# Layer 2's forget queries and keys by column blocks, with two smaller moves to ScalarE

## The chip, the cores and the metric

One core of a Trainium2 chip runs the whole program. The metric is the device time of one execution in microseconds (us). Engine names are those of the profile: PE multiplies matrices, PEld loads its stationary operand, DVE is the vector engine, ACT the scalar engine, POOL the general-purpose one, SP the queue from which transfers are issued.

## The reference, cut to what matters

Two layers on 256 tokens of 1024 features, in single precision. Each layer has a mixer with two groups of eight heads (sparse attention with grouped keys, and forgetting attention), then a squared-ReLU MLP; each is wrapped in norms.

```python
h = _rms_norm(x, g_pre_mix[l])
parts = jnp.split(h @ w_in[l], split_at, axis=-1)
nq, kc, vc, ksel, vsel, kwin, vwin, gates, fq, fk, fv, ff = parts
o_nsa = _nsa_mixer(...)                       # compressed, selected and window branches, gated
o_fox = _fox_mixer(heads(fq, 8), heads(fk, 8), heads(fv, 8), ff, b_forget[l])
mix = jnp.concatenate([o_nsa, o_fox], axis=-1) @ w_out[l]
x = x + _rms_norm(mix, g_post_mix[l])
h = _rms_norm(x, g_pre_mlp[l])
y = jnp.square(jax.nn.relu(h @ w_up[l])) @ w_down[l]
x = x + _rms_norm(y, g_post_mlp[l])
```

In the forgetting group, a head's logits are `q . k / 8 + cum[q] - cum[k]` under a causal mask, where `cum` is the running sum of log-sigmoids of `ff`; softmax of them multiplies `fv`. `fq` and `fk`, 512 columns each of `w_in`, are what the change is mostly about.

## The kernel before, in words

**Products in three parts.** Every large product of `h` and a weight is made of three matmuls. `Weights.get` brings a weight unit of 128 x 1024 numbers (tile `wraw`), and splits it into a rounded high part `whi` (a copy by ACT) and a low part `wlo` (a subtraction by DVE). The activations lie turned (features on partitions) as `xT`, also a high and a low part, side by side in one tile: `xT[0]` high, `xT[1]` low, `xT[2]` both, 2 x 256 columns for each of the eight feature groups k. A product is high x high + high x low + low x high (`mm3`).

**The input projection** goes chunk by chunk through `w_in` (`CHUNKS`): 0 to 2 and 5 are made with tokens on partitions (`in_chunk`), chunk 3 (`fq`) and chunk 4 (`fk`) turned, features on partitions, by `in_chunk_T`. There the weights are the stationary operand and `xT` the moving one. A chunk's four units hold two k-steps each; at every k-step the four blocks of 128 columns get their three matmuls of 256 columns, into two PSUM tiles `acc` of two blocks each. At the end of the chunk DVE multiplies both tiles with the row scale `T["r"]` into `T[name]`, `fqT` or `fkT`. There are two `acc` buffers, three `s`, two `x` and one `o`. The MLP's `up` already works in another form: block by block, a high weight against `xT[2]` (512 columns), then the low weight against `xT[0]` (256 columns), into one `s` tile; ACT copies one half of it and DVE adds the other.

**Attention.** A loop over 24 head parts (`flat`) for each layer: in step i it makes the scores of part i (`scores`: product, masked maximum by DVE, exponential by ACT), scales part i - 1 by the reciprocal of its sum (`scale`), turns part i - 2 (`probs_T`: three transposes of PE into an `s` tile, and a copy to `prT` or `prX`, by DVE for even i and by ACT for odd i), and multiplies with V for pairs that are complete (`pv`). Between these stand shares of the remaining chunks of the input projection and of the output projection: `fill` takes one or more shares from the generator `stream`, up to each `yield`.

**The norms.** `sandwich` adds a normed result to `X`. `rsqrt_sum` makes the inverse root from two partial sums of squares: y by a logarithm and an exponential on ACT, a correction t = -0.5 b + d by DVE, and two more steps by DVE. In the last norm of layer 2 nothing follows but the addition to `X` and the store.

**Order.** All instructions are recorded first (`Recorder`). `schedule` then lays them out engine by engine with costs (`_cost`, `_latency`), buffers as they come free, and ranks; `order` does so several times, with due times from the pass before (`deadlines`), and keeps the best. Instructions of `in_chunk_T`'s end get the rank of the chunk's begin (`nc.key = begin`). So an edit at one place can shift the order elsewhere. Every instruction of the program is issued from one line of `emit`, which is why the profile names L410 nearly everywhere, and groups are told apart by their tiles. Transfers leave in the order of SP's queue.

Of the kernel before, what the change touches and what calls it, by code (L numbers as in the profile page):

```python
# [20 lines left out]
AF = mybir.ActivationFunctionType  # L21
OP = mybir.AluOpType
PSUM = bass.MemoryType.PSUM

P = 128
D = 1024
S = 256
NT = 2
DEPTH = 2
# [24 lines left out]
EPS = 1e-6  # L54

CHUNKS = [(512, 1024), (1024, 1312), (0, 512), (1312, 1824), (1824, 2336), (2336, 2848)]
SEGS = ((0, 128, 0), (128, 384, 1))
GELU_C = 1.5957691216057308

# [472 lines left out]
def trunk(nc, A, consts_in, out, sbp, pp, dram):  # L532
# [12 lines left out]
    def add_unit(key, shape, src, kind="split"):  # L545
        index[key] = len(units)
        units.append((kind, shape, src))
# [5 lines left out]
    RIDES = {}  # L553
# [4 lines left out]
    for l in range(DEPTH):  # L558
        at = 0
        for c, (a, b) in enumerate(CHUNKS):  # L560
            w_in = A["w_in"][l][:, at:at + 8 * (b - a)].rearrange("p (k n) -> p k n", k=8)
            at += 8 * (b - a)
            for q, (k0, k1) in enumerate(parts_of(l, c)):
                add_unit((l, "in", c, q), [k1 - k0, b - a], w_in[:, k0:k1, :])
                if (c, q) in RIDES:
                    s, j = RIDES[c, q]
                    w1 = A["cmp_w1_" + s][l].rearrange("p (k n) -> p k n", k=16)
                    add_unit((l, "w1" + s, j), [4, 256], w1[:, 4 * j:4 * j + 4, :], "raw")
        wo = A["w_out"][l].rearrange("(k p) n -> p k n", p=P)
        for k in range(8):  # L570
            add_unit((l, "out", k), [1, D], wo[:, k:k + 1, :])
        wu0 = A["w_up0"][l].rearrange("p (k n) -> p k n", k=8)
        wd = A["w_down"][l].rearrange("(k p) n -> p k n", p=P)

        def up_units(fc):
            for q in range(4):
                if fc:
                    add_unit((l, "up", fc, q), [8, P], A["w_up"][l, 4 * (fc - 1) + q])
                else:
                    add_unit((l, "up", fc, q), [2, 512], wu0[:, 2 * q:2 * q + 2])  # L580

        up_units(0)
        for fc in range(8):
            if fc < 7:
                up_units(fc + 1)
            for q in range(4):
                add_unit((l, "dn", fc, q), [1, D], wd[:, 4 * fc + q:4 * fc + q + 1, :])
# [18 lines left out]
    for k in range(8):  # L606
# [8 lines left out]
        a = 8 + k * NFIRST - o  # L615
# [19 lines left out]
    ps = psum("o")  # L635
# [36 lines left out]
        nc.scalar.activation(dst[0], src, AF.Copy)  # L672
        nc.vector.tensor_sub(dst[1], src, dst[0].bitcast(F32))

    def rsqrt_sum(a, b, eps=EPS):

        w = small([P, 5], "rsqrt", 6)
        c, d, y, t, r = (w[:, i:i + 1] for i in range(5))
        nc.vector.tensor_scalar(c, a, eps, None, op0=OP.add)
        nc.vector.tensor_scalar(d, c, -0.5, None, op0=OP.mult)  # L680
        nc.scalar.activation(y, b, AF.Ln, bias=c)
        nc.scalar.activation(y, y, AF.Exp, scale=-0.5)
        nc.vector.tensor_scalar(t, b, -0.5, d, op0=OP.mult, op1=OP.add)
        nc.vector.scalar_tensor_tensor(t, y, t, y, op0=OP.mult, op1=OP.mult)
        nc.vector.scalar_tensor_tensor(r, t, 1.5, y, op0=OP.add, op1=OP.mult)
        return r
# [32 lines left out]
    def sandwich(t, acc, g_post, pre=None, xT=None, eps=EPS, store=None):  # L719


        sq = small([P, 2], "sq")
# [7 lines left out]
        for n in range(2):  # L730
# [3 lines left out]
                mg[n] = times("mg", n, pre[0])  # L734
            if n == 0 and not pre:
                m[0] = times("m", 0, g_post)
        r = rsqrt_sum(sq[:, 0:1], sq[:, 1:2], eps)
        if not pre:
            m[1] = times("m", 1, g_post)
        if pre:  # L740
            xg = []
            for n in range(2):
                xg.append(mg[n])
                for c in (0, 256):
                    a = n * 512 + c
# [6 lines left out]
        for n in range(2):  # L752
            if pre:
                m[n] = times("m", n, g_post)
            nc.vector.scalar_tensor_tensor(X[t][:, half(n)], m[n], r, X[t][:, half(n)],
                                           op0=OP.mult, op1=OP.add)
# [21 lines left out]
    xT = new_xT()  # L778
# [13 lines left out]
    for l in range(DEPTH):  # L792
# [10 lines left out]
        T = {}  # L803
# [286 lines left out]

        def in_chunk_T(c, name):

            begin = len(nc.ops)
            ps = [psum("acc") for _ in range(2)]
            for q, (k0, k1) in enumerate(parts_of(l, c)):
                w = weight(l, "in", c, q)
                for k in range(k0, k1):
                    for b in range(4):
                        mm3(ps[b // 2][:, (b % 2) * S:(b % 2) * S + S], [y[:, k - k0, b * P:b * P + P] for y in w],
                            [y[:, k, :] for y in xT[:2]], k == 0 and b % 2 == 0, k == 7, check=False)  # L1100
                        if b % 2:
                            yield
                if (c, q) in RIDES:
                    hidden_part(*RIDES[c, q])
                    yield
            T[name] = qT_tile(name)
            nc.key = begin
            for b in range(2):
                nc.vector.tensor_mul(T[name][:, 2 * b:2 * b + 2, :], ps[b].rearrange("p (b n) -> p b n", b=2),
                                     T["r"][:, None, :].to_broadcast([P, 2, S]))  # L1110
            nc.key = None
            yield
# [225 lines left out]
        for i in range(len(flat) + 4):  # L1338
# [11 lines left out]
                side[i]()  # L1350
                fill(1)
            if 0 <= i - 2 < len(flat):
                pTs[flat[i - 2]] = probs_T(st.pop(i - 2)[0], i % 2, flat[i - 2])
            fill(1)
            j = i - 3
            if 0 <= j < len(flat) and flat[j][2] == 1 and flat[j][3] != 1:
# [173 lines left out]
def layouts(a):  # L1530
# [4 lines left out]

    rows_of = lambda w: w.reshape(DEPTH, -1, P, w.shape[2]).transpose(0, 2, 1, 3).reshape(DEPTH, P, -1)
    w = r["w_in"]
    r["w_in"] = np.concatenate([rows_of(w[:, :, a:b]) for a, b in CHUNKS], axis=2)
    for k in ("cmp_w1_k", "cmp_w1_v"):
        r[k] = rows_of(r[k])  # L1540
    u = r.pop("w_up")
# [30 lines left out]
```

## Time and profile before

| | |
|---|---|
| median of 3 runs | 621.98 us (621.16 to 622.2) |
| profiled execution | 622.06 us, span 620.0 us |
| granted TensorE clock | 0.998 |
| PE | 612.1 us busy (99%), 3558 matmuls |
| PEld | 518.5 us (84%) |
| DVE | 474.2 us (76%), 1039 instructions |
| ACT | 379.6 us (61%), 726 instructions |
| POOL | 9.3 us (2%) |
| read from memory | 117.15 MB |

A time row of the profile gives start, duration, engine, line, operation, `out<-in` by tile names and the shape; a group row gives the count, the busy time in us, the mean in ns, and the idle time of the engine before them with what ended it. Matmuls overlap, so the distance between two starts tells what one costs, not its duration. Single-precision products that are no transposes appear as two records for each instruction. Layer 1's input projection and attention lie from about 5 to 122 us, its output projection and MLP up to about 305 us, and layer 2 follows in the same way.

### The profile page before, as it was taken

The numbers are of one execution on the slowest core, as the hardware profiler recorded it, in microseconds if no ns is written. First come the engines' busy times: TensorE is split into PE (matmuls) and PEld (weight loads), VectorE is DVE, ScalarE is ACT, GpSimd is POOL, SyncE is SP. The second block draws the span as 40 slices with busy tenths as digits, with TensorE's granted clock in tenths as the row PEclk, the third lists the DMA queues.
The fourth block names the chain that finished last, engine by engine and source line by source line (L and its number), as shares of the span: only waits on it lengthen the run. The fifth ranks groups of instructions, "written<-read, shape, count | busy, mean of one in ns | idle before, by whom it ended". The sixth has DMA issues, their size and how long they took to land.

```text
span 620.0 us, 9981 instructions
## 1 busy us (share of the span) xinstructions
PE 612.1 (99%) x3558; PEld 518.5 (84%) x3558; DVE 474.2 (76%) x1039; ACT 379.6 (61%) x726; POOL 9.3 (2%) x20
## 2 busy tenths in 40 slices
PE   9999999999999999999999999999999999999995
PEld 7989987788888888888888998777888888888884
DVE  6889999889976567557598999997996576566534
ACT  6767677577655456545466747775776456456522
POOL 0001100000000000000000020000000000000000
PEclk9999999999999999999999999999999999999999
DMA  8996637518765565564346783453486555555001
GB/s 321 403 345 211 238 108 248 185 56 301 257 193 186 189 199 196 188 194 139 107 138 242 276 297 101 169 191 118 127 299 206 188 199 175 198 201 177 30 1 69
DMA packets 34818, 118.87 MB, mean 192 GB/s; under 512 B 4144, under 2 KB 4304, under 8 KB 34768
## 3 DMA queue, kind: packets, MB, share of 16 engines
q1 hardware_dynamic: 34768, 118.23, 56.5%
q8 instruction: 28, 0.46, 0.3%
q14 instruction: 22, 0.18, 0.1%
HBM read 117.15 MB, written 1.07 MB: 191 GB/s over the span
## 4 chain that ended last, share of the span: by engine, by line
PE 99%; DVE 0%; issue 0%; DVEq 0%; ACT 0%
PE s L410 35%; PE acc L410 31%; PE x L410 25%; PE o L410 7%; DVE x L410 0%; DVE m L410 0%; DVEq L1568 0%; DVE rsqrt L410 0%; ACT rl L410 0%; DVEq L410 0%
## 5 line engine op out<-in xcount | busy, mean ns | idle before, releaser
L410 DVE TENSOR_TENSOR wlo<-wraw,whi 128x1024 fp32r<-128x1024 f32 (+1 forms) x188 | 225.7, 1203 | 96.2 <-ACT whi L410 56.2
L410 ACT ACTIVATE whi<-wraw 128x1024 fp32r<-128x1024 f32 (+1 forms) x188 | 195.1, 1042 | 112.1 <-PE acc L410 76.8
L410 PE MATMUL s<-xT,whi 128*128 128x512 f32 x448 | 106.5, 390 | 0.0
L410 PEld LDWEIGHTS s<-xT,whi 128*128 128x128 f32 x448 | 83.3, 188 | 16.8
L410 PE MATMUL x<-whi,aT 128*128 128x512 f32 x256 | 88.6, 390 | 0.0
L410 PE MATMUL acc<-whi,aT 128*128 128x512 f32 x256 | 88.3, 389 | 0.0
L410 PEld LDWEIGHTS s<-xT,wlo 128*128 128x128 f32 x448 | 57.4, 191 | 2.2
L410 PE MATMUL s<-xT,wlo 128*128 128x256 f32 x448 | 58.1, 283 | 0.0
L410 PEld LDWEIGHTS acc<-whi,aT 128*128 128x128 f32 x256 | 48.0, 188 | 10.0
L410 PEld LDWEIGHTS x<-whi,aT 128*128 128x128 f32 x256 | 48.1, 188 | 9.5
L410 PE MATMUL x<-wlo,aT 128*128 128x512 f32 x128 | 50.0, 390 | 0.0
L410 ACT ACTIVATE pr<-pr,st 128x256 f32<-128x256 f32 (+1 forms) x96 | 42.7, 447 | 11.8 <-DVE st L410 11.4
L410 PE MATMUL acc<-wlo,aT 128*128 128x512 f32 x128 | 49.9, 390 | 0.0
L410 PE MATMUL acc<-xT,whi 128*128 128x256 f32 x256 | 49.6, 287 | 0.0
L410 PEld LDWEIGHTS acc<-xT,whi 128*128 128x128 f32 x256 | 40.6, 190 | 1.6 <-issue 0.8
L410 PE MATMUL acc<-whi,xT 128*128 128x512 f32 (+1 forms) x128 | 36.8, 352 | 0.0
L410 PE MATMUL acc<-xT,wlo 128*128 128x256 f32 x128 | 36.3, 284 | 0.0
L410 PE MATMUL x<-whi,xT 128*128 128x512 f32 x112 | 36.1, 399 | 0.0
L410 ACT ACTIVATE h<-s 128x256 f32<-128x256 f32 x56 | 21.2, 378 | 16.0 <-PE s L410 16.0
L410 ACT ACTIVATE rl<-h 128x512 f32<-128x512 f32 x28 | 17.7, 633 | 18.6 <-DVE h L410 18.6
L410 PEld LDWEIGHTS acc<-wlo,aT 128*128 128x128 f32 x128 | 24.0, 188 | 5.0
L410 PEld LDWEIGHTS x<-wlo,aT 128*128 128x128 f32 x128 | 24.1, 188 | 4.5
(216 smaller groups left out, 952.6 us busy)
## 6 DMA issues: line engine op xcount, KB each, us to landing
wraw<-in_w_up_dram SPq DMA_DIRECT2D x64, 512.0 KB, 4.0
wraw<-in_w_down_dram SPq DMA_DIRECT2D x64, 512.0 KB, 4.0
wraw<-in_w_in_dram SPq DMA_DIRECT2D x36, 512.0 KB, 4.7
wraw<-in_w_out_dram SPq DMA_DIRECT2D x16, 512.0 KB, 4.4
w<-in_cmp_w_k_dram SPq DMA_DIRECT2D x8, 512.0 KB, 5.2
w<-in_cmp_w_v_dram SPq DMA_DIRECT2D x8, 512.0 KB, 5.0
bias<-sums SPq DMA_DIRECT2D x8, 384.0 KB, 6.8
first<-in_first_dram SPq DMA_DIRECT2D x7, 384.0 KB, 5.3
```

What stands on the lines that cost most here:

```text
L410: getattr(getattr(self.nc, op.engine), name)(*[real(v) for v in args], **{k: real(v) for k, v in kw.items()})
```

## The change

1. In layer 2 alone (`TURNED`), chunks 3 and 4 are made block by block. A weight unit now holds all eight k-steps of one block of 128 columns; the host lays the weights out so (`by_columns`), at the same size. For a block, eight matmuls take the high weight against both parts of x (512 columns), then eight the low weight against the high part (256 columns, into the second half of the tile). ACT copies the second half, DVE adds the first, and after every second block DVE multiplies two blocks with the row scale. Each block has an `acc` tile of its own. Layer 1 keeps the old form as `in_chunk_T1`.
2. `probs_T` always copies by ACT.
3. In the last norm of layer 2 (`store` is given there alone) the step t of `rsqrt_sum` is an ACT operation with scale -0.5 and d as its addend.

```diff
--- before.py
+++ after.py
@@ -54,6 +54,7 @@
 EPS = 1e-6
 
 CHUNKS = [(512, 1024), (1024, 1312), (0, 512), (1312, 1824), (1824, 2336), (2336, 2848)]
+TURNED = ((1, 3), (1, 4))
 SEGS = ((0, 128, 0), (128, 384, 1))
 GELU_C = 1.5957691216057308
 
@@ -560,8 +561,12 @@
         for c, (a, b) in enumerate(CHUNKS):
             w_in = A["w_in"][l][:, at:at + 8 * (b - a)].rearrange("p (k n) -> p k n", k=8)
             at += 8 * (b - a)
+            turned = w_in.rearrange("p k n -> p (k n)").rearrange("p (b k n) -> p b k n", b=4, n=P) if (l, c) in TURNED else None
             for q, (k0, k1) in enumerate(parts_of(l, c)):
-                add_unit((l, "in", c, q), [k1 - k0, b - a], w_in[:, k0:k1, :])
+                if (l, c) in TURNED:
+                    add_unit((l, "in", c, q), [8, P], turned[:, q])
+                else:
+                    add_unit((l, "in", c, q), [k1 - k0, b - a], w_in[:, k0:k1, :])
                 if (c, q) in RIDES:
                     s, j = RIDES[c, q]
                     w1 = A["cmp_w1_" + s][l].rearrange("p (k n) -> p k n", k=16)
@@ -672,7 +677,7 @@
         nc.scalar.activation(dst[0], src, AF.Copy)
         nc.vector.tensor_sub(dst[1], src, dst[0].bitcast(F32))
 
-    def rsqrt_sum(a, b, eps=EPS):
+    def rsqrt_sum(a, b, eps=EPS, last=False):
 
         w = small([P, 5], "rsqrt", 6)
         c, d, y, t, r = (w[:, i:i + 1] for i in range(5))
@@ -680,7 +685,10 @@
         nc.vector.tensor_scalar(d, c, -0.5, None, op0=OP.mult)
         nc.scalar.activation(y, b, AF.Ln, bias=c)
         nc.scalar.activation(y, y, AF.Exp, scale=-0.5)
-        nc.vector.tensor_scalar(t, b, -0.5, d, op0=OP.mult, op1=OP.add)
+        if last:
+            nc.scalar.activation(t, b, AF.Identity, scale=-0.5, bias=d)
+        else:
+            nc.vector.tensor_scalar(t, b, -0.5, d, op0=OP.mult, op1=OP.add)
         nc.vector.scalar_tensor_tensor(t, y, t, y, op0=OP.mult, op1=OP.mult)
         nc.vector.scalar_tensor_tensor(r, t, 1.5, y, op0=OP.add, op1=OP.mult)
         return r
@@ -734,7 +742,7 @@
                 mg[n] = times("mg", n, pre[0])
             if n == 0 and not pre:
                 m[0] = times("m", 0, g_post)
-        r = rsqrt_sum(sq[:, 0:1], sq[:, 1:2], eps)
+        r = rsqrt_sum(sq[:, 0:1], sq[:, 1:2], eps, store is not None)
         if not pre:
             m[1] = times("m", 1, g_post)
         if pre:
@@ -1090,6 +1098,38 @@
 
         def in_chunk_T(c, name):
 
+            if (l, c) not in TURNED:
+                yield from in_chunk_T1(c, name)
+                return
+            T[name] = qT_tile(name)
+            for b in range(4):
+                begin = len(nc.ops)
+                hi, lo = weight(l, "in", c, b)
+                ps = psum("acc")
+                for k in range(8):
+                    nc.tensor.matmul(ps, hi[:, k, :], xT[2][:, k].rearrange("p j n -> p (j n)"), start=k == 0, stop=False,
+                                     skip_group_check=True)
+                    if k % 4 == 3:
+                        yield
+                for k in range(8):
+                    nc.tensor.matmul(ps[:, S:], lo[:, k, :], xT[0][:, k, :], start=False, stop=k == 7,
+                                     skip_group_check=True)
+                    if k % 4 == 3:
+                        yield
+                if (c, b) in RIDES:
+                    hidden_part(*RIDES[c, b])
+                    yield
+                nc.key = begin
+                d = T[name][:, b, :]
+                nc.scalar.activation(d, ps[:, S:], AF.Copy)
+                nc.vector.tensor_add(d, ps[:, :S], d)
+                if b % 2:
+                    d = T[name][:, b - 1:b + 1, :]
+                    nc.vector.tensor_mul(d, d, T["r"][:, None, :].to_broadcast([P, 2, S]))
+                nc.key = None
+            yield
+
+        def in_chunk_T1(c, name):
             begin = len(nc.ops)
             ps = [psum("acc") for _ in range(2)]
             for q, (k0, k1) in enumerate(parts_of(l, c)):
@@ -1350,7 +1390,7 @@
                 side[i]()
                 fill(1)
             if 0 <= i - 2 < len(flat):
-                pTs[flat[i - 2]] = probs_T(st.pop(i - 2)[0], i % 2, flat[i - 2])
+                pTs[flat[i - 2]] = probs_T(st.pop(i - 2)[0], 1, flat[i - 2])
             fill(1)
             j = i - 3
             if 0 <= j < len(flat) and flat[j][2] == 1 and flat[j][3] != 1:
@@ -1535,7 +1575,11 @@
 
     rows_of = lambda w: w.reshape(DEPTH, -1, P, w.shape[2]).transpose(0, 2, 1, 3).reshape(DEPTH, P, -1)
     w = r["w_in"]
-    r["w_in"] = np.concatenate([rows_of(w[:, :, a:b]) for a, b in CHUNKS], axis=2)
+
+    by_columns = lambda x: x.reshape(DEPTH, P, 8, 4, P).transpose(0, 1, 3, 2, 4).reshape(DEPTH, P, -1)
+    ins = [rows_of(w[:, :, a:b]) for a, b in CHUNKS]
+    r["w_in"] = np.stack([np.concatenate([by_columns(x)[l] if (l, c) in TURNED else x[l] for c, x in enumerate(ins)], axis=1)
+                          for l in range(DEPTH)])
     for k in ("cmp_w1_k", "cmp_w1_v"):
         r[k] = rows_of(r[k])
     u = r.pop("w_up")
```

## The prediction

> **What bounds the kernel now.** I read the page first: the span, the busy shares and the chain that ended last.
>
> ```profile
> span 620.0 us, 9981 instructions
> PE 612.1 (99%) x3558; PEld 518.5 (84%) x3558; DVE 474.2 (76%) x1039; ACT 379.6 (61%) x726; POOL 9.3 (2%) x20
> PE 99%; DVE 0%; issue 0%; DVEq 0%; ACT 0%
> ```
>
> PE carries 99% of the chain. A busy PE can still hide waits, because its ends are modelled, so I looked at the starts of matmuls instead. The chain in order of time gives two stretches, and the view of PE's waits (weight loads) gives those that DVE or ACT ended: eight rows that add up to 3.4 us of the whole span.
>
> ```profile
> 165.64 11.11 PE s L410 x64
> 350.86 6.11 PE acc L410 x51
> ```
>
> ```profile
> PEld s L410 <- DVE st L410: 1.1, 3, 0.4
> ...
> PEld x L410 <- DVE wlo L410: 0.4, 1, 0.4
> PEld acc L410 <- DVE wlo L410: 0.4, 1, 0.4
> PEld s L410 <- ACT pr L410: 0.4, 1, 0.4
> PEld o L410 <- DVE wlo L410: 0.4, 1, 0.4
> PEld acc L410 <- ACT pr L410: 0.3, 1, 0.3
> PEld x L410 <- ACT xT L410: 0.2, 1, 0.2
> PEld s L410 <- DVE pr L410: 0.2, 1, 0.2
> ```
>
> The first stretch is four blocks of an up projection, 32 matmuls of 512 columns and 32 of 256, and it takes the same 11.11 us each time it occurs. The second is 51 matmuls of 256 columns from the middle of layer 2's forget q: 6.11 / 51 = 0.120 us each, with no hole between them. So PE issues without a pause, and the kernel's time is a sum of issue steps, plus a head and a tail. An edit pays if it shortens PE's own list or the tail, and costs if it makes PE wait.
>
> Next, how full are the engines that feed PE? The table by stretches, for the attention stage of layer 1 (32 to 122) and of layer 2 (340 to 425):
>
> ```profile
> core 0: us, PE busy (x) PEld busy (x) DVE busy (x) ACT busy (x) POOL busy (x), PEclk, DMA share, GB/s
> 32.00:122.00 90.00, 89.94 (x683) 74.64 (x682) 84.99 (x267) 62.87 (x158) 4.61 (x8) 1.00 0.64 219
> 340.00:425.00 85.00, 85.00 (x664) 70.96 (x662) 79.65 (x259) 57.93 (x151) 4.50 (x8) 1.00 0.59 199
> ```
>
> DVE is at 94% in both, ACT at 70% and 68%; PE still does not wait for them. The granted clock is 1.00, so it is no term.
>
> **Part 1: forget q and k of layer 2 by column blocks.** Before, each of the two chunks has 8 k-steps x 4 blocks x 3 products, 96 matmuls of 256 columns. By the second stretch that is 96 x 6.11 / 51 = 11.50 us. After, a block takes 8 matmuls of 512 columns (the high part of the weights against both parts of x) and 8 of 256: for four blocks just the mix of the first stretch, 11.11 us. To see whether a 512-column step is as short among attention work, PE's timeline:
>
> ```profile
> 382.90 0.62 PE L410 MATMUL acc<-whi,xT 128*128 128x512 f32 x2
> ...
> 385.41 0.49 PE L410 MATMUL s<-cst,pr 128*128 128x128 f32 x3
> ...
> 395.21 0.82 PE L410 MATMUL s<-cst,pr 128*128 128x128 f32 x6
> 395.79 0.47 PE L410 MATMUL acc<-whi,xT 128*128 128x512 f32 x1
> 396.10 0.39 PE L410 MATMUL acc<-wlo,xT 128*128 128x512 f32 x1
> ```
>
> Between 382.90 and 385.41 lie 11 matmuls of 512 columns: 2.51 / 11 = 0.228 us each. Then 32 x 0.228 + 32 x 0.120 = 11.14, which confirms 11.11. The saving is 0.39 us for a chunk, **0.78 us for both**. A pair of 256 costs 0.240 and one of 512 costs 0.228: what goes is a fixed part of some 12 ns in each of 64 pairs.
>
> The Trainium skill, "TensorE: Matmul & The Clock Gate", section "Back-to-back issue gap", speaks against this size: it gives a warm step as N / 2.4 + 2.5 ns, which puts the fixed part at 2.5 ns, and as an estimate by that page the 64 pairs would save 0.16 us. The rows above differ from it (0.120 and 0.228 against its 0.109 and 0.216), so the measurement decides.
>
> The last three rows show a second price. After single-precision transposes the next rounded matmul starts its successor 0.31 us later (395.79 to 396.10) instead of 0.23: 0.08 us for each return. Counted in the order of PE's instructions, the rounded stream is left 88 times before and 91 times after, because a few transposes and score products that stood side by side now stand apart. Three returns cost **+0.25 us**. Otherwise PE's order in layer 2 stays as it was, with the same attention pieces between the same shares of a chunk.
>
> **Part 2: what the blocks add beside PE.** The groups by line:
>
> ```profile
> L410 DVE TENSOR_TENSOR fqT<-acc,rT 128x512 f32<-128x512 f32 x4 | 2.8, 692 | 0.1
> L410 DVE TENSOR_TENSOR h<-s,h 128x256 f32<-128x256 f32 x56 | 21.3, 417 | 0.4 <-ACT h L410 0.2
> L410 ACT ACTIVATE h<-s 128x256 f32<-128x256 f32 x56 | 21.2, 378 | 16.0 <-PE s L410 16.0
> L410 DVE TENSOR_TENSOR h<-rl 128x512 f32<-128x512 f32 x28 | 19.0, 684 | 0.0
> L410 DVE COPY prT<-s 128x384 f32<-128x384 f32 x16 | 8.8, 550 | 0.1
> L410 DVE COPY prX<-s 128x384 f32<-128x384 f32 x8 | 4.4, 552 | 0.1
> L410 ACT ACTIVATE prT<-s 128x384 f32<-128x384 f32 x16 | 7.7, 483 | 3.0 <-PE s L410 2.9
> ```
>
> A chunk loses two DVE products out of PSUM (2 x 0.69 = 1.38) and gains four ACT copies like h<-s (4 x 0.378 = 1.51), four DVE sums like h<-s,h (1.67) and two products (1.37). For both chunks: DVE +3.3, ACT +3.0 us. The weight units keep their size and number; a unit now serves one block of 2.78 us instead of two k-steps of 2.88 us, so loads and splits fall due at the same pace, and the low parts even later, after eight matmuls of the high part. Price on PE: nothing, while the covers below hold. The parameter load and two or three weight loads swap places on SP's queue, each far ahead of its use.
>
> **Part 3: turned probabilities.** The 24 copies that DVE made (16 + 8, 12 in each layer) go to ACT: DVE -12 x 0.55 = -6.6, ACT +12 x 0.483 = +5.8 us a layer. Loads after: layer 1 DVE 84.99 - 6.6 = 78.4 of 90 (87%), ACT 62.87 + 5.8 = 68.7 (76%); layer 2 DVE 79.65 - 6.6 + 3.3 = 76.4 of 85 (90%), ACT 57.93 + 5.8 + 3.0 = 66.7 (78%). The fuller engine gets relief and the other stays below what DVE bears today without holding PE. So: nothing on the path. If that cover went, each late copy would hold back the product with V by what ACT has queued ahead; that is the first rival.
>
> **Part 4: a step of the last norm.** The tail, from the timeline:
>
> ```profile
> 613.49 0.19 ACT L410 ACTIVATION_READ_ACCUMULATOR rl<-acc 128x1 f32 x1
> 613.72 0.69 DVE L410 TENSOR_TENSOR m<-acc,gains 128x512 f32<-128x512 f32 x1 [1.81 <-ACT rl L410]
> 613.72 0.29 ACT L410 ACTIVATE rsqrt<-sq,rsqrt 128x1 f32<-128x1 f32 x1
> 614.04 0.20 ACT L410 ACTIVATE rsqrt<-rsqrt 128x1 f32<-128x1 f32 x1
> 614.33 0.20 DVE L410 TENSOR_SCALAR rsqrt<-sq,rsqrt 128x1 f32<-128x1 f32 x1
> 614.63 0.41 DVE L410 SCALAR_TENSOR_TENSOR rsqrt<-rsqrt 128x1 f32<-128x1 f32 x2
> ```
>
> Today the step t sits on DVE behind the product m: it starts at 614.33 and the next step at 614.63, while ACT's logarithm and exponential ended at 614.24. In the changed order t is an ACT operation, ahead of the exponential with the logarithm. Its nearest row is the logarithm, also one element with a per-row addend: from its start to the next 614.04 - 613.72 = 0.32. The exponential then runs to about 614.56, and DVE follows 0.04 later (as m follows the accumulator's read, 613.68 to 613.72), at 614.60. With a t as short as the exponential (0.20) it would be 614.48, with 0.45 it would be 614.73: **-0.15 to +0.10, taken -0.03 us**. On the first token half the same swap lies under matmuls.
>
> **The sum.** -0.78 + 0.25 - 0.03 = **-0.56 us**. The profiled execution took 622.06 us (span 620.0 and 2.1 around it) and the median of the three runs is 621.98, so they can stand for each other: 621.98 - 0.56 = **621.4 us**.
>
> **Rivals.** *ACT becomes the late one (slower).* A block's PSUM buffer comes free only when ACT's copy and then DVE's sum are done: 0.378 + 0.417 = 0.80 us, and there are two such buffers, so PE asks for it again one block, 11.11 / 4 = 2.78 us, later. That leaves 1.98 us for what stands ahead on ACT, whose queue is in order. Rows like these stand there:
>
> ```profile
> 351.48 2.01 ACT L410 ACTIVATE whi<-wraw 128x1024 fp32r<-128x1024 f32 x2
> ...
> 353.52 0.50 ACT L410 ACTIVATE pr<-pr,st 128x256 f32<-128x256 f32 x1
> ```
>
> Two splits alone already fill the cover. With a small copy (0.38) between them PE would wait 0.4 us, with an exponential besides 0.9; at four of the eight hand-overs (six blocks and the start of the next chunk's two) that is 1.6 to 3.6, say 2.6 us: 621.4 + 2.6 = **624.0**. Behind a waiting sum on DVE stand the next low split and the row maxima, so the delay would spread. It decides once ACT runs 2 us behind. Against it: attention pieces of PE lie between the blocks and lengthen the cover, ACT has a fifth of its time free, and MLP blocks with the same copies keep 11.11. Chance 0.12.
>
> *Relief of DVE shows (faster).* Of the 3.4 us that weight loads waited, DVE ended 2.5 us (the five rows with DVE). If half of these were real waits of PE and went, 621.4 - 1.25 = **620.2**. Against it: the starts of matmuls show no such holes; weight loads run ahead. Chance 0.07.
>
> *The wide matmuls bring nothing (no change).* If the fixed part does not go when narrow products with other weights stand between, only the switches are left: 621.98 + 0.25 = **622.2**. By the page above it would be 622.0 or so. The row of 11 steps at 0.228 speaks against it. Chance 0.15.
>
> My forecast keeps 0.66.
>
> **How the numbers follow.** About 0.2% (1.2 us) is what a measurement of this kernel can tell from no change; the three runs lie 1.0 us apart. Forecast and third rival fall inside, with 0.01 of the forecast lost to each side by the runs' own spread: same 0.79. Faster 0.08, slower 0.13. The range takes the forecast with the spread of the runs and the tail's bounds, and reaches toward both outer cases: 620.6 to 623.2; beyond it stay most of the slower case and some of the faster, under 0.2.
>
> **What would show it.** Right: in layer 2 stretches of 8 wide and 8 narrow acc matmuls in 2.78 us, 64 matmuls fewer, a copy of turned probabilities on ACT only, DVE near 90% and ACT near 78% there, the last chain step on DVE 0 to 0.1 us earlier after the last matmul. Wrong: starts of acc matmuls with holes over 0.1 us at a block's first product, waits of PE for ACT's copies of fqT, fkT or prT, or wide steps at 0.24.

## The result, and the profile after

| | before | after |
|---|---|---|
| median | 621.39 us (22 runs, 621.16 to 622.24) | 620.53 us (22 runs, 620.36 to 621.05) |
| profiled execution, span | 622.06 us, 620.0 us | 620.53 us, 618.4 us |

The ratio is 0.9986, with a 95% interval of 0.998 to 0.9992: a gain of 0.86 us, between 0.50 and 1.24. The forecast was 621.4, with a range from 620.6 to 623.2, so the measured time lies 0.07 us below that range. The three runs of before that were known then had a median of 621.98; 22 runs put it at 621.39.

First, the page of the changed kernel: span, busy shares and the chain that ended last.

```profile
span 618.4 us, 9854 instructions
PE 611.0 (99%) x3494; PEld 514.6 (83%) x3494; DVE 465.3 (75%) x1021; ACT 388.9 (63%) x760; POOL 10.8 (2%) x20
PE 99%; DVE 0%; DVEq 0%; issue 0%; ACT 0%
```

PE is still the chain, with 64 matmuls fewer (3494 for 3558). Next the table by stretches for the two attention stages (start and end, length, then busy time and count of PE, PEld, DVE, ACT and POOL, the granted clock, the transfers' share and rate).

```profile
32.00:122.00 90.00, 90.00 (x684) 75.08 (x683) 79.78 (x255) 66.63 (x170) 5.97 (x8) 1.00 0.67 229
340.00:425.00 85.00, 85.00 (x601) 68.16 (x600) 77.14 (x255) 63.81 (x172) 4.61 (x8) 1.00 0.61 208
```

DVE was forecast at 78.4 and 76.4 us and has 79.8 and 77.1; ACT at 68.7 and 66.7 and has 66.6 and 63.8. PE is busy through both. A block of a turned chunk, in PE's timeline of after (the first row ends the block before it):

```profile
350.56 1.11 PE L411 MATMUL acc<-xT,wlo 128*128 128x256 f32 x8
351.51 2.00 PE L411 MATMUL acc<-xT,whi 128*128 128x512 f32 x8
353.35 1.11 PE L411 MATMUL acc<-xT,wlo 128*128 128x256 f32 x8
```

Eight narrow steps take 0.95 us and eight wide ones 1.84, so 0.119 and 0.230 each, and 2.79 us for a block; 2.78 was forecast. The copy of turned probabilities is on ACT alone:

```profile
L411 ACT ACTIVATE prT<-s 128x384 f32<-128x384 f32 x32 | 14.9, 485 | 2.9 <-PE s L411 2.7
```

Last, the tail of after, from its last matmul:

```profile
611.45 0.39 PE L411 MATMUL acc<-whi,aT 128*128 128x512 f32 x1
...
612.60 0.69 DVE L411 TENSOR_TENSOR m<-acc,gains 128x512 f32<-128x512 f32 x1 [1.72 <-ACT rl L411]
612.60 0.48 ACT L411 ACTIVATE rsqrt<-sq,rsqrt 128x1 f32<-128x1 f32 x2
612.98 0.19 ACT L411 ACTIVATE rsqrt<-rsqrt 128x1 f32<-128x1 f32 x1
613.20 0.41 DVE L411 SCALAR_TENSOR_TENSOR rsqrt<-rsqrt 128x1 f32<-128x1 f32 x2
```

DVE's step that needs the exponential starts 0.60 us after m (613.20 - 612.60). Before, it was 0.91 (614.63 - 613.72). That is -0.31 us where -0.03 was forecast.

### The profile page after: what moved, and what is told of

Read it like the earlier page. It is cut to its first block, busy times and chain, and to the rows that moved or that the text cites. A ratio compares the mean times of both kernels' runs of the same rounds, so it can differ in the third digit from the quotient of the medians.

```text
span 618.4 us, 9854 instructions
## 1 busy us (share of the span) xinstructions
PE 611.0 (99%) x3494; PEld 514.6 (83%) x3494; DVE 465.3 (75%) x1021; ACT 388.9 (63%) x760; POOL 10.8 (2%) x20
## 4 chain that ended last, share of the span: by engine, by line
PE 99%; DVE 0%; DVEq 0%; issue 0%; ACT 0%
PE s L411 35%; PE acc L411 31%; PE x L411 25%; PE o L411 7%; DVE x L411 0%; DVE m L411 0%; DVEq L1612 0%; DVE rsqrt L411 0%; ACT rl L411 0%
## 5 line engine op out<-in xcount | busy, mean ns | idle before, releaser
L411 PE MATMUL acc<-xT,whi 128*128 128x256 f32 (+1 forms) x192 | 42.4, 324 | 0.0
L411 PEld LDWEIGHTS acc<-xT,whi 128*128 128x128 f32 x192 | 31.7, 190 | 3.3 <-issue 0.8
L411 PE MATMUL acc<-xT,wlo 128*128 128x256 f32 x128 | 28.6, 286 | 0.0
L411 ACT ACTIVATE rl<-x 128x512 f32<-128x512 f32 x24 | 14.6, 610 | 22.2 <-PE x L411 18.0
```

What stands on the lines that cost most here:

```text
L411: getattr(getattr(self.nc, op.engine), name)(*[real(v) for v in args], **{k: real(v) for k, v in kw.items()})
```

## Experiments

In the notes below, "layer 2" is the time from the first product of the compressed keys in layer 2 (`o<-w,kstk`) to the first wide product of its MLP (`s<-xT,whi`); a single profiled execution gives it without what differs in the head and in the landing of the last store. The stretch from the same product in layer 1 to that in layer 2 is called "layer 1". Two executions with one list for PE, before and norm_only, differ by 0.08 us in layer 2 (106.51 and 106.43), and four with after's list lie between 106.09 and 106.19, so differences of 0.1 us say nothing. Ratios are against runs of the kernel before on the same chip.

### The parts one at a time

**norm_only**: step t on ACT, nothing else.

```diff
-TURNED = ((1, 3), (1, 4))
+TURNED = ()
...
-                pTs[flat[i - 2]] = probs_T(st.pop(i - 2)[0], 1, flat[i - 2])
+                pTs[flat[i - 2]] = probs_T(st.pop(i - 2)[0], i % 2, flat[i - 2])
```

> The kernel before with the step of the last norm on ACT alone; the order of PE's instructions is the one of before. Theory (the norm's step is worth 0.3 us by itself: ACT does it in the wait between the logarithm and the exponential that depends on it, and DVE no longer has it behind the product m): from the start of the last product m to the start of DVE's next step 0.60 us as in the changed kernel, against 0.91 before; about 0.3 us off the time. Rival (that gain comes with the other two edits or is chance of one execution): 0.91 stays, no change in time. My prediction's term of 0.03 us would give 0.88.

**no_norm**: blocks and copies without the norm's step.

```diff
-        r = rsqrt_sum(sq[:, 0:1], sq[:, 1:2], eps, store is not None)
+        r = rsqrt_sum(sq[:, 0:1], sq[:, 1:2], eps)
```

> The changed kernel with the norm's step back on DVE; PE's order is the one of the changed kernel. Theory: PE's stretches as in the changed kernel (layer 2's attention 91.05), the tail as before (0.91 from m to the next step, 7.4 us from the last matmul's start to the end), so 0.3 us slower than the changed kernel and 0.6 faster than before. Rival (the tail is shorter for another reason): the tail stays at 0.60 and 7.0.

**blocks_only**: no_norm, with the copies as before (`i % 2`).

> The kernel before with layer 2's two chunks by column blocks alone. Theory (a sum of PE's steps): by the order, the rounded stream is left 90 times against 88, so -0.78 us for the two chunks and about -0.1 to +0.2 for the new order: from the first kstk product of layer 2 to the first single-precision transpose of its MLP some 0.4 to 0.8 us less than 91.47, last matmul's start to the end 7.4 us as before; time -0.6 to -0.8 us. Rival (the wide steps bring nothing): the stretch keeps 91.5.

**copies_only**: no_norm with `TURNED = ()`.

> The kernel before with all turned probabilities copied by ACT alone. Theory (PE never waited, so relief of DVE is worth nothing; only the new order of PE counts): 89 exits of the rounded stream against 88, 0.1 to 0.3 us more, within what a measurement can tell. Rival (DVE's relief let PE run without small waits, which is where layer 1's 0.25 us came from): layer 1's attention and MLP 0.25 us shorter, and time 0.2 to 0.5 us less.

Measured, as medians against the kernel before:

| kernel | us | before | ratio, 95% interval |
|---|---|---|---|
| norm_only | 621.17 | 621.48 | 0.9992 (0.9983 to 1.0001) |
| no_norm | 620.92 | 621.48 | 0.999 (0.9981 to 0.9999) |
| blocks_only | 622.26 | 621.48 | 1.0011 (1.0002 to 1.002) |
| copies_only | 621.74 | 621.48 | 1.0002 (0.9994 to 1.0011) |

By the medians the norm's step gives -0.31 and the two other edits together -0.56. That this adds up so well to the -0.86 of the whole is in part luck: each interval is over 1 us wide, and that of norm_only reaches no change, so the evidence for the norm's step is the rows of its tail. Blocks alone lose 0.78, and copies alone gain nothing (+0.26, with an interval that includes no change), so these two are not additive. The first and last rows of layer 2, in the timelines of norm_only, after, copies_only and blocks_only:

```profile
340.18 1.93 PE L411 MATMUL o<-w,kstk 128*32 128x256 f32 x32
446.61 3.79 PE L411 MATMUL s<-xT,whi 128*128 128x512 f32 x16
```

```profile
340.16 1.93 PE L411 MATMUL o<-w,kstk 128*32 128x256 f32 x32
446.26 3.79 PE L411 MATMUL s<-xT,whi 128*128 128x512 f32 x16
```

```profile
340.17 1.93 PE L411 MATMUL o<-w,kstk 128*32 128x256 f32 x32
447.32 3.79 PE L411 MATMUL s<-xT,whi 128*128 128x512 f32 x16
```

```profile
340.16 1.93 PE L411 MATMUL o<-w,kstk 128*32 128x256 f32 x32
447.67 3.79 PE L411 MATMUL s<-xT,whi 128*128 128x512 f32 x16
```

That is 106.43, 106.10 (-0.33), 107.15 (+0.72) and 107.51 (+1.08) us. Layer 1 took 306.75 to 306.77 in all four, so nothing happens there. The profiled execution of copies_only (622.00 us) lies 0.26 above the median of its runs, so its +0.72 may be more than is usual. Where do these two lose? blocks_only waits at the norm between the mixer and the MLP (its PE timeline):

```profile
432.76 0.39 PE L411 MATMUL acc<-whi,oT 128*128 128x512 f32 x1
433.33 1.54 PE L411 MATMUL s<-cst,mg 128*128 128x128 f32 x8 [0.18 <-DVE mg L411]
434.76 0.50 PE L411 MATMUL s<-whi,xT 128*128 128x512 f32 x1
435.09 0.40 PE L411 MATMUL s<-wlo,xT 128*128 128x512 f32 x1
435.68 0.73 PE L411 MATMUL s<-whi,xT 128*128 128x512 f32 x2 [0.19 <-DVE rsqrt L411]
```

The last product of the output projection (432.76) comes before all eight `s<-cst,mg`, and then PE has nothing left to do but wait. DVE was not behind with its work: shortly before, in its timeline, it stood idle for 2.07 us (until 426.78) and 0.66 us (until 428.13). In after, output products stand between and behind the two groups of four, and cover the norm:

```profile
431.21 0.60 PE L411 MATMUL s<-cst,mg 128*128 128x128 f32 x4
431.57 0.48 PE L411 MATMUL acc<-wlo,oT 128*128 128x512 f32 x1
431.88 0.60 PE L411 MATMUL s<-cst,mg 128*128 128x128 f32 x4
432.24 0.71 PE L411 MATMUL acc<-whi,oT 128*128 128x512 f32 x2
```

copies_only waits once, for DVE's low part of `pcs`, which is 0.53 of its 0.72 us (its timeline; PE's step before the second row's product is 0.65 us instead of 0.12):

```profile
370.66 0.28 PE L411 MATMUL acc<-xT,wlo 128*128 128x256 f32 x1
371.31 0.34 PE L411 MATMUL s<-identr,pcs 128*128 128x128 f32 x2 [0.37 <-DVE pcs L411]
```

Two theories could explain that the edits help together and not apart. *Load*: the blocks fill DVE (81.1 of 85 us in blocks_only), so the copies have to leave it. *Order*: each edit makes the planner lay out another list for PE, and what is gained or lost lies in where that list leaves PE without work.

### Where copies go

**copies_l2**: after, with ACT's copies in layer 2 alone (`l or i % 2`).

> The changed kernel, with all turned probabilities on ACT in layer 2 alone; layer 1 alternates as before. Theory (load in layer 2 is what the copies are for; layer 1 gains nothing from them): layer 1 306.8 us from its first kstk product to that of layer 2, less 26.7, as in all kernels whose layer 1 is not by blocks; layer 2 as in the changed kernel, 106.1; time that of the changed kernel within 0.1%. Rival (layer 1's copies bring part of the gain): layer 1 0.2 us longer than in the changed kernel. Second rival (order): layer 2 differs from 106.1 by more than 0.2.

620.38 us against 621.41, ratio 0.9984 (0.9975 to 0.9993); layer 2 takes 106.08 and layer 1 306.75. Layer 1's twelve moved copies bring nothing. This is the fastest kernel of the study, though it can't be told from after.

**blocks_odd**: blocks alone, with the odd copies on DVE (`1 - i % 2`). **blocks_pool**: blocks alone, the product with the row scale by POOL (`nc.gpsimd.tensor_mul`). **both_layers**: after with `TURNED = ((0, 3), (0, 4), (1, 3), (1, 4))`. **both_pool**: both_layers with POOL's product.

> Blocks alone, with the alternation of the turned probabilities the other way round: DVE copies the odd ones, ACT the even ones. The load of both engines is that of blocks alone. Theory (load): 107.2 to 107.6 us from the first kstk product of layer 2 to its first up product, with waits of about 1 us at the norm before the MLP. Rival (order): the waits are elsewhere or gone, 106.0 to 106.8.

> Blocks alone, but the two products with the row scale of each chunk on POOL instead of DVE (2.7 us off DVE in layer 2); the turned probabilities alternate as before, and the norm's step is on DVE. Theory (load: blocks alone put DVE of layer 2's attention stage at 95%, the last products with V come late, and PE has no filler left at the norm between mix and MLP): with that load off, PE's waits at the MLP's first turned tiles (1.2 us in blocks alone) go, and from the first kstk product of layer 2 to its first up product the kernel takes 106.0 to 106.4 us, against 107.5 with blocks alone and 106.4 with the norm edit alone. Rival (order: any edit reshuffles PE's instructions and the waits are chance): anything from 106.0 to 107.6, no relation to DVE's load.

> The changed kernel with layer 1's two chunks by column blocks as well. Theory (sum of PE's steps; 96 exits against 91): -0.78 us for layer 1's chunks, +0.1 to +0.4 for five exits: 0.4 to 0.7 us less than the changed kernel. Rival (layer 1's engines are fuller, so PE will wait for the blocks' evacuation): holes over 0.1 us at the blocks' first products, and no gain.

> The changed kernel with layer 1's chunks by blocks too, and the products with the row scale on POOL in both layers. Theory (load): both layers by blocks alone lost layer 1's gain in small waits and 0.35 us at the norm before layer 2; with 2.7 us less on DVE in each layer these go, and layer 1 takes 0.4 to 0.7 us less than the changed kernel's; time 0.4 to 0.6 us under the changed kernel. Rival (order): no gain over both layers by blocks, about 621.2.

| kernel | us | before | ratio, 95% interval | layer 2 |
|---|---|---|---|---|
| blocks_odd | 622.86 | 621.41 | 1.0022 (1.0014 to 1.0031) | 107.43 |
| blocks_pool | 622.16 | 621.41 | 1.0012 (1.0003 to 1.0021) | 107.26 |
| both_layers | 621.25 | 621.52 | 0.9996 (0.9987 to 1.0005) | 106.15 |
| both_pool | 623.63 | 621.41 | 1.0036 (1.0023 to 1.0048) | 107.33 |

Three lists with blocks and half of the copies on DVE lose 0.8 to 1.1 us in layer 2, as the load theory wants. In blocks_pool the waits at the norm are gone, and a single one of 1 us is left, again for `pcs`, where POOL disturbed DVE (last section). Without it layer 2 would take 106.3 us, as the load theory forecast; but its list was planned anew too, so it does not tell the theories apart. In both_layers, layer 2 keeps its gain and layer 1 gains nothing of the 0.4 to 0.7 us that were expected: its first `s<-cst,mg` comes at 127.32 us, against 127.28 in after, and at the norm ahead of layer 2 eight such transposes take 1.29 us (314.16 to 315.45), 0.16 each for 0.09 in after, so that layer 2 begins at 340.69 instead of 340.16. In blocks_odd it begins at 340.91, so its list loses in layer 1 as well. These five left load and order open.

### PE's list of one kernel, the copies' engine of another

The order of all instructions was planned as in the parent kernel, and only then the 24 even copies changed their engine. PE's list is the parent's to the last instruction. The diff shows the swap from ACT to DVE; the swap from DVE to ACT is made in the same way.

```diff
-            for op in self.order():
+            for op in [o.swapped() for o in self.order()]:
...
+    def swapped(self): self.engine, self.name, self.args = self.swap or (self.engine, self.name, self.args); return self
...
+                nc.scalar.activation(pT, ps[:, :384], AF.Copy); nc.ops[-1].swap = ("vector", "tensor_copy", (pT, ps[:, :384])) if swap else None
```

**after_dve**: after's list, even copies by DVE.

> The changed kernel with the order of every engine's other work kept, PE's list of instructions unchanged to the last, and only the 24 turned copies of even parts carried out by DVE instead of ACT. DVE then has 77.1 + 6.6 = 83.7 us of work in the 85 us of layer 2's attention. Load theory (the copies must leave DVE because the blocks fill it): PE waits return and layer 2, from its first kstk product to the MLP's first product, takes 106.8 to 107.3 us instead of 106.1; median 621.2 to 621.7. Order theory (what costs is the order in which PE's list was laid out): 106.1 to 106.3, median 620.4 to 620.7.

**blocks_act**: blocks_only's list, even copies by ACT.

> The blocks alone (no norm step), with PE's list as it was in blocks_only, and the 24 turned copies of even parts carried out by ACT. Load theory: with DVE 6.6 us lighter the waits at the norm go, layer 2 falls from 107.5 to 106.2 to 106.5 us and the median from 622.3 to 621.0 to 621.3. Order theory: the list that ends its out-projection products before the norm stays, so do its waits; 107.2 to 107.6, median 622.0 to 622.4.

**copies_dve**: copies_only's list, even copies by DVE.

> The copies alone (no blocks, no norm step): PE's list as it was planned for copies on ACT, but the even ones carried out by DVE again. Load theory: more work on DVE, so layer 2 is as long as in copies_only or longer, 107.1 to 107.8 us; median 621.7 to 622.3. Order theory: the wait at the pcs products belongs to the list; 107.0 to 107.3, median 621.6 to 621.9. If the wait came from a chance collision of POOL and DVE, it goes: 106.4 to 106.6, median 621.0 to 621.2.

**norm_act**: norm_only's list, even copies by ACT.

> The norm step with the list of PE of the kernel before, and all turned copies carried out by ACT. Load theory: DVE is 6.6 us a layer lighter and PE never waited for it, so nothing or a gain of up to 0.2: layer 2 106.2 to 106.4 us, median 621.0 to 621.2. Order theory: 106.4 as in norm_only, median 621.1 to 621.2. If the copies in themselves cost PE time (later exits from ACT), 106.6 or more and 621.4 or more.

| kernel | us | before | ratio, 95% interval | layer 2 (parent) |
|---|---|---|---|---|
| after_dve | 624.11 | 621.62 | 1.004 (1.0027 to 1.0053) | 107.27 (106.10) |
| blocks_act | 622.77 | 621.62 | 1.0018 (1.0009 to 1.0027) | 107.77 (107.51) |
| copies_dve | 625.76 | 621.62 | 1.0067 (1.0054 to 1.0079) | 108.64 (107.15) |
| norm_act | 621.88 | 621.62 | 1.0004 (0.9995 to 1.0013) | 106.86 (106.43) |

In layer 2 all four take longer than their parents. In norm_act twelve copies fewer on DVE in each layer, in a list where PE never waited for DVE, cost 0.43 us. Two places hold nearly all of it. At 370.77 us, 0.18 us: ACT makes a moved copy `prT` (369.70) ahead of its own part of `pcs`, DVE stands idle for 0.69 us until that is done, and PE waits for DVE. At 402.46, 0.24 us: PE's next transposes start only when ACT's copy `prX`, behind a split of 1.05 us, has ended. So copies on ACT can hold PE, as the third band of that note had it. The table by stretches of blocks_only, and then of blocks_act:

```profile
340.00:425.00 85.00, 85.00 (x594) 68.23 (x594) 81.09 (x266) 59.51 (x159) 4.29 (x8) 1.00 0.59 199
```

```profile
340.00:425.00 85.00, 84.97 (x590) 67.83 (x589) 76.25 (x254) 63.93 (x171) 4.23 (x8) 1.00 0.60 199
```

DVE falls from 81.1 to 76.3 us, below after's 77.1, and the same two waits stand at the norm (timeline of blocks_act):

```profile
433.79 1.54 PE L411 MATMUL s<-cst,mg 128*128 128x128 f32 x8 [0.17 <-DVE mg L411]
...
436.14 0.73 PE L411 MATMUL s<-whi,xT 128*128 128x512 f32 x2 [0.19 <-DVE rsqrt L411]
```

So at a fixed list, relieving DVE takes nothing visible off the blocks' loss. This alone proves nothing, because the moved copies have a price of their own, 0.43 us in norm_act, and a relief of that size could hide in it. Two other pairs are cleaner, because their traces hold the same instructions on the same engines and differ in order alone. blocks_act and no_norm both have 3494 records on PE, 1023 on DVE and 758 on ACT: layer 2 takes 107.77 us in one and 106.09 in the other, and the medians are 622.77 and 620.92 (621.62 and 621.48 for the kernel before on their chips). copies_dve and before both have 3558, 1039 and 726: layer 2 takes 108.64 and 106.51 us, and the medians are 625.76 and 621.62. So with equal work on every engine the order is worth up to 4 us, and the load theory, which knows only the work, falls.

The order theory in its bare form, that PE's list alone fixes the time, falls too: it wanted 106.1 to 106.3 for after_dve. No kernel came wholly as either theory said. after_dve is in the load theory's band in layer 2 and 2.4 us above its band in the median; blocks_act is a little above the band of the order theory, and copies_dve above all. In layer 1, where the load of after_dve and copies_dve is that of the kernel before, they lose 2.2 and 1.9 us. What the kernels show is a fit of both: under a list that was planned for one choice of engines, a copy that moves to another queue stands there ahead of work that PE needs. The steps of PE that grew most against after lie all over the stage (in after_dve 0.54 us at 95.15, 0.30 at 114.01, 0.20 at 399.04). The largest can be followed in the timelines of DVE and PE:

```profile
94.89 0.55 DVE L411 COPY prX<-s 128x384 f32<-128x384 f32 x1
95.36 0.41 DVE L411 CUSTOM_DVE_ANT_0 pr<-x,cst 128x256 f32<-128x256 f32 x1
95.93 0.47 PE L411 MATMUL x<-whi,oT 128*128 128x512 f32 x1 [0.39 <-DVE st L411]
```

The moved copy stands ahead of a masked maximum that reads an `x` tile, and PE's next product into `x` starts only behind that. In after two such maxima follow each other without the copy between them (92.86 and 93.21), and PE goes on without a wait. That is the pattern of norm_act, with DVE and ACT exchanged. At the other places it was not followed which copy holds back which product.

### The tail

**exp_first**: the exponential ahead of the step, both still on ACT.

```diff
-        nc.scalar.activation(y, b, AF.Ln, bias=c)
-        nc.scalar.activation(y, y, AF.Exp, scale=-0.5)
+        nc.scalar.activation(t if last else y, b, AF.Ln, bias=c)
+        nc.scalar.activation(y, t if last else y, AF.Exp, scale=-0.5)
```

> The changed kernel, but ACT does the norm's step behind the exponential, not between it and the logarithm (the logarithm goes through the step's place, which the exponential reads before the step may overwrite it). PE's order as in the changed kernel. Theory (the step fills ACT's wait between two dependent operations): the exponential waits for the logarithm as before, 0.32 us from start to start, and the step comes after: 0.75 to 0.80 from the start of m to DVE's next step, against 0.60 in the changed kernel and 0.91 before. Rival (what counts is only that DVE no longer has the step behind m): 0.60 to 0.65 again.

**dve_t_first**: the step back on DVE, but ahead of m: it takes its d from the tile of m, so that m has to follow.

> The changed kernel with the norm's step back on DVE, but ahead of the product m instead of behind it (d is kept in m's own tile, which m overwrites). PE's order as in the changed kernel. Theory (with the step on ACT, both engines work side by side): DVE now has the step and then m, so its next step comes when m is nearly done: 0.75 to 0.85 us after the step's start, against 0.60 and 0.91. Rival (it is the place behind m alone that costs; ACT has no part in it): 0.60 to 0.65.

620.91 us (ratio 0.9989, 0.9981 to 0.9998) and 620.86 (0.9988, 0.9979 to 0.9997), both against 621.52. The tail of exp_first in its timeline:

```profile
612.81 0.29 ACT L411 ACTIVATE rsqrt<-sq,rsqrt 128x1 f32<-128x1 f32 x1
612.81 0.69 DVE L411 TENSOR_TENSOR m<-acc,gains 128x512 f32<-128x512 f32 x1 [1.85 <-ACT rl L411]
613.13 0.20 ACT L411 ACTIVATE rsqrt<-rsqrt 128x1 f32<-128x1 f32 x1
613.37 0.29 ACT L411 ACTIVATE rsqrt<-sq,rsqrt 128x1 f32<-128x1 f32 x1
613.70 0.41 DVE L411 SCALAR_TENSOR_TENSOR rsqrt<-rsqrt 128x1 f32<-128x1 f32 x2 [0.20 <-ACT rsqrt L411]
```

DVE goes on 0.89 us after m began, where 0.75 to 0.80 was expected and before had 0.91. So -0.02: nearly my forecast of -0.03, which had put the three ACT operations in a row, each waiting for the one ahead. (By this edit the step does have to wait for the exponential, whose input it overwrites.) The gain needs the step *between* the two others. In this kernel the exponential starts 0.32 after the logarithm, for whose result it waits. In after it starts 0.38 later (612.60 to 612.98), although a whole operation was put between: the step does not need the logarithm and starts 0.20 after it, while that one still runs, and the exponential starts 0.18 after the step:

```profile
612.80 0.28 ACT L411 ACTIVATE rsqrt<-sq,rsqrt 128x1 f32<-128x1 f32 x1
```

It adds 0.06 us there, not 0.32. dve_t_first confirms that DVE's queue is the other half: with the step ahead of m, DVE goes on 0.86 us after the logarithm began (612.92 to 613.78; 0.75 to 0.85 was expected), held back by m, which now starts at 613.17.

### The price of a return to rounded products

**switches**: seven visits of single-precision transposes added in each MLP, one transpose at a time in layer 1 and three in layer 2.

```diff
+                if b == 2:
+                    spare = psum("o")
+                    with nc.stretch():
+                        for i in range(1 if l == 0 else 3):
+                            nc.tensor.transpose(spare[:, i * P:i * P + P], ident, ident)
```

> The changed kernel with extra single-precision transposes into a spare PSUM tile that nobody reads: in seven of the up projections of layer 1 one at a time, in seven of layer 2 three at a time. The result is not touched. Theory (each exit from the rounded stream costs a fixed 0.08 to 0.1 us beside the transposes' own steps): one alone costs 0.11 to 0.14 us, three 0.33 to 0.36. Rival (the price belongs to each transpose): one costs a third of three.

624.33 us, 1.0043 (1.0028 to 1.0058). From its first `s<-cst,mg` to the next layer's first product, layer 1's second half took 213.72 us (127.96 to 341.68) for 212.88 in after (127.28 to 340.16): 0.12 for each visit of one. In layer 2, from there to the last matmul, it took 182.55 (432.75 to 615.30) for 180.24 (431.21 to 611.45): 0.33 for each visit of three. These are the numbers that the theory asked for, but the rival asks for nearly the same ones, a third of 0.33. The slope decides: two transposes more cost 0.21, so one costs 0.105, and 0.015 is left for the visit. PE's timeline shows one alone:

```profile
176.70 0.27 PE L411 MATMUL o<-cst 128*128 128x128 f32 x1
176.72 0.47 PE L411 MATMUL x<-whi,aT 128*128 128x512 f32 x1
177.04 0.39 PE L411 MATMUL x<-wlo,aT 128*128 128x512 f32 x1
```

From the transpose to the second product lie 0.34 us, 0.11 more than the 0.23 of the product alone. The longer step after a transpose (0.31 for 0.23) is paid back by the last transpose, whose own step is shorter by as much (0.03 for 0.11). One of the seven visits in each layer stands right behind the transposes `s<-cst,h` and only lengthens their visit, at the same price. All this holds for transposes; visits of other single-precision products were not added.

## Why the prediction was right and wrong

**Baseline: wrong by 0.59.** The sum stood on 621.98, the median of three runs; 22 runs give 621.39. Of the miss of 0.89 us (621.42 against 620.53) this is the larger part. The execution that was profiled, which seemed to confirm the base, was a long one too: against norm_only, which has the same list for PE, its first `o<-w,kstk` comes 0.43 us later (33.86 for 33.43), and two steps before `pcs` are 0.22 and 0.09 longer. The change was forecast at -0.56 and measured at -0.86. That the range began only 0.8 below the forecast, with half a microsecond of doubt in the base alone, made it too narrow.

**Part 4, the norm's step: the mis-sized term.** The mechanism, t leaving the place behind m, was right. Taken at -0.03 within -0.15 to +0.10, it measured -0.31 in the traces, with the same -0.31 in the medians of norm_only (-1.06 to +0.06). The step that failed is "Its nearest row is the logarithm": the 0.32 us from the logarithm to the exponential was charged for both distances, from the logarithm to t and from t to the exponential. But that pair is one in which the second waits for the first. Where nothing is waited for the distances are 0.20 and 0.18 us, so DVE went on 0.60 after m and not 0.88. The Trainium skill, "ScalarE: Activation LUTs", section "What ACT_TABLE_LOAD costs", says that activations which follow each other overlap by about 93 ns; that agrees with the row of after, where two operations that don't depend on each other (0.29 and 0.28) span 0.48 us, an overlap of 0.09.

**Part 1, chunks: right, a little large; the returns: right by luck.** -0.78 was forecast. The sum of PE's steps that start with a product of `acc<-xT,whi` in layer 2 falls from 16.03 us (128 in norm_only) to 15.26 (64 in after), and that of `acc<-xT,wlo` rises from 7.85 to 7.98: -0.64. The 0.16 us that came from the Trainium skill's "Back-to-back issue gap" (in "TensorE: Matmul & The Clock Gate") is a quarter of what these steps show; that section gives the rule for an isolated matmul, and this is a stream of them. Against the three returns, +0.25, stand +0.30 in the rest of layer 2, so the net is -0.33 in one trace, and -0.56 (-1.18 to -0.06) in the medians of no_norm, for -0.53 forecast. The size fits, but the reason does not: a return from transposes has no price to speak of (0.015 by switches). What the rows show to cost is another kind of visit. In PE's timelines of after, and then of norm_only:

```profile
405.04 0.51 PE L411 MATMUL acc<-wlo,oT 128*128 128x512 f32 x1
405.48 0.87 PE L411 MATMUL o<-prT,vS 128*64 128x256 f32 x8
```

```profile
405.19 0.93 PE L411 MATMUL s<-fkT,fqT 64*128 64x128 f32 x8
406.04 0.44 PE L411 MATMUL o<-prT,vS 128*64 128x256 f32 x2
```

In after an output product stands alone between score products and products with V, and its step takes 0.44 us instead of 0.23; a second one at 413.88 takes 0.43. In norm_only scores and V products follow each other directly at both places. These two steps alone are +0.41, and the rest of layer 2 nets to -0.1. No run varied this by itself. In both_layers the same stands in layer 1 too (101.14 and 109.98, 0.43 us each), which is a part of why it gained nothing there.

**Parts 2 and 3, "nothing on the path": right as a sum, wrong as parts.** No block waited and ACT was never late, so the first rival had no ground, and the second neither: moved copies in layer 1 bring nothing. But apart from each other neither edit is free. I had taken it that an engine below the load that PE bears today cannot hold PE back. The runs show that load decides little here: with DVE at 79.1 of 85 us in layer 2's attention PE loses 2.1 us in layer 2 if the list was not laid out for it (copies_dve), and with the same work at 79.7, as before, it does not.

**Third rival.** Wide matmuls do bring what their steps promised, so it falls.

## What to carry to other kernels

Where two small dependent operations follow each other on one engine, a third that neither of them needs can stand between them almost for free (0.06 us here), so read the price of an operation from independent neighbours and not from a dependent pair. Where a planner lays out the order, edits can't be priced one by one (blocks alone lost, copies alone gained nothing, both together won): measure the whole, and to tell load from order compare kernels with the same work on the same engines in different order. Price a switch by the slope over visits of different length, not by the one step that looks long, and for the kind of product that is switched to.

## What the runs showed of the hardware

POOL can slow DVE. In blocks_pool, while POOL multiplies (its timeline):

```profile
369.35 1.29 POOL L411 TENSOR_TENSOR fkT<-fkT,rT 128x512 f32<-128x512 f32 x1 [1.76 <-DVE fkT L411]
...
369.53 1.93 DVE L411 TENSOR_TENSOR pcs<-cs,pcs 128x256 fp32r<-128x256 f32 x2
...
371.07 0.34 PE L411 MATMUL s<-identr,pcs 128*128 128x128 f32 x2 [0.83 <-DVE pcs L411]
```

This pair of DVE subtractions took 0.76 us in norm_only and in after. Here the first alone took 1.39, ending 0.28 after POOL's product, and PE waited for it. In copies_only the same happens under POOL's mask operation:

```profile
369.05 1.84 POOL L411 TENSOR_SCALAR_AFFINE_SELECT bias<-bias 128x256 f32<-128x256 f32 x2 [1.38 <-ACT whi L411]
...
369.20 1.42 DVE L411 TENSOR_TENSOR wlo<-wraw,whi 128x1024 fp32r<-128x1024 f32 x1
370.55 0.95 DVE L411 TENSOR_TENSOR pcs<-cs,pcs 128x256 fp32r<-128x256 f32 x2
```

The low split takes 1.22 us in the median, and 1.42 here; the first subtraction takes 0.62 instead of 0.42. Over the traces of thirteen kernels (all but switches and the four exchanged ones), the scaling of `pr` (128 x 256, in SBUF) has a median of 0.41 us without POOL beside it and 0.50 where POOL is busy for over half of it; the masked maximum that reads PSUM (`pr<-x,cst`) has 0.42 and 0.41. Not every overlap shows: 35 low splits under POOL have the usual median of 1.22. The Trainium skill, "SBUF — State Buffer", section "Who interferes with whom", states the rule: a DVE operation with two inputs in SBUF contends with a POOL operation that reads SBUF, over ports that only one of them can hold. The rows of blocks_pool agree; by the 35 splits it does not bind in every overlap, or POOL's spans are too rough to tell. The scaling has only one such input and slows all the same. POOL's product itself took 1.28 to 2.34 us for 128 x 512 in its four occurrences in blocks_pool, against 0.68 on DVE, so moving this product to POOL was no relief.
